# A hybrid decoder layer on one core: the first modulation sums on VectorE, gate rows from transposed tiles, sigmoid through tanh, and a new order of instructions

## The chip, the cores and the metric

The kernel runs on one core of one Trainium2 chip. The metric is the device time of one execution in microseconds (us); lower is better. Engines are named as in the profile: PE is TensorE's matrix multiply (PEld its weight load), DVE is VectorE, ACT is ScalarE, POOL is GpSimd, SP the engine that issues the loads.

## The reference, cut to what matters

One decoder layer in float32, with 512 tokens of width 1024 and one conditioning vector c of width 1024:

```python
mod = silu(c) @ ada_w + ada_b                      # 6 x 1024
sh1, sc1, g1, sh2, sc2, g2 = split(mod, 6)
h = rms_norm(x, pre_norm_mix) * (1 + sc1) + sh1
y = hybrid_mixer(h, ...)                           # input projection, RG-LRU group, sparse attention group, output projection
x = x + (1 + g1) * rms_norm(y, post_norm_mix)
h = rms_norm(x, pre_norm_mlp) * (1 + sc2) + sh2
x = x + (1 + g2) * rms_norm(relu(h @ w_ff1) ** 2 @ w_ff2, post_norm_mlp)
# inside the RG-LRU group, elementwise per channel and token, xc = causal conv of a projection of h:
r, i = sigmoid(xc @ wa + ba), sigmoid(xc @ wx + bx)      # block-diagonal weights
log_a = -8 * r * softplus(-lam)
u = sqrt(-expm1(2 * log_a)) * (i * xc)                   # then the scan h_t = exp(log_a) * h_(t-1) + u_t
```

## The kernel before, in words

Nearly all products are float32 through fp32r: each operand is split into a high and a low part (`hi`, `lo`), and three products replace one (`mm3`). VectorE, ScalarE and POOL make these parts, so they are busy throughout.

**Opening** (`first_wave`, `norm_x`, `ada_load`, `ada_sums`). Four loads bring x, 128 tokens each. ScalarE sums the squares, POOL makes the root, and x is scaled in pieces. `sil`, the silu of c, is broadcast to all partitions by eight small plain fp32 products with `ident` and two copies; the result is `silb`. Sixteen loads bring the tiles of `ada_w` for shift and scale, two per block of 128 channels. For block j `ada_sums` makes a shift and a scale column (`sa`): for j = 0 (`PE_SUMS = 1`) by 16 one-column products on TensorE, for the others by `tensor_tensor_reduce` on VectorE, multiplying the transposed tile by `silb` and summing along the row. Then four transposes, the modulated tile on ScalarE (`hh`, and once more `hf`), the low part `hl` on VectorE, and 18 products of 512 columns into six banks. So the first wave is eight blocks, each with two sums on VectorE. `WARM` plain products on x stand in TensorE's queue before it.

**Middle.** Projections for the RG-LRU and the queries, the compressed keys, and attention run interleaved. `gates` makes r and i (sigmoid on ScalarE out of PSUM); `vector_work` runs the convolution, the decay (tanh, exponential, square root), the scan, the gelu and the group's norm. `ada_row` makes the row (1 + g) * gain for the residual: per half of 512 columns `ada_sum` accumulates eight row tiles, each scaled by a column of `sil`, into `accT` on VectorE; POOL adds the bias on one partition; a product with `ones` sums over the partitions; VectorE multiplies by the gain. It runs for g1 beside the attention and for g2 (stream `G2`) beside the first MLP product.

**End.** `turn_h` and `up_first`, the up projection (`up`, partly by a Strassen scheme), the down projection (`down_all`) with the last residual.

**What sets the order.** Every operation is recorded as a node in the order in which the generator functions make it, then `flush` issues all of them in the order of `PLAN`, a string with one position per node. Each engine works through its own queue in that order. Where an operation may run on several engines, the letter of `PLACE` says which (a ScalarE, d VectorE, p POOL). `TABLES` (line 54) lists which activation tables hold a function: tanh in those of exp, sigmoid and gelu, sigmoid only in its own. In the profile most operations have a helper's line: L334 products, L337 transposes, L344 activations, L376 VectorE and POOL operations, L418 loads.

Of the kernel before, what the change touches and what calls it, by code (L numbers as in the profile page):

```python
# [14 lines left out]
P = 128  # L15
S = 512
# [21 lines left out]
WARM = 16  # L38
# [7 lines left out]
OPENING = "0123AAwAAwAA"  # L46

PE_SUMS = 1
# [27 lines left out]
    '-4-;-=-@-C+?+@,>,L,8,<,:,j-E-F-I+B+C+d+v+r+~+e+l,}-*---K-9-]-^-g-5-J-L-N-P-Q-V-X-Y-f-j-~.0.4.;.@.h-6'
    '-:->-R-W-a-A-T-}..-Z-[-_-c-e-n-q-r-t.b/</W,H,J,X,],O,U-v-x-|+{,#,&,a.$.(.*.-./.6.^.l/y.?.A.E.F.P.Q.Z'
    '.v/&04/b0*01-`.#.,.1.3.8.H.~//-p-y.&.5.M.U.9.:.V.j,e,f-M-h-O-m,;,K-G-b-s-w/+-z.)-{.+.>.W.e.k.m.o.{/:'
    '/c/p-d-i-u.%.2.B-l-o.7.R.i.q.r.s/)/8.t.x.y/5/?/F.<.=.J.g._.u.D.G.L.n.}/./U/Z/6/2/1/>/A/B/J/K/D/H/Y/_'
    '/N/`/f/h.|/(/,/I/4/C.d.f.p.z/k/n0-0S0U/O/P/^/e/m0:/l/o/r/t0D0N/=/@/Q/]/L/T/%/0/S/g/q/{0?0(0//}0@0>/~'  # L80
    '0H0f0g0a0c0m0s0h0p0r0t/a/w0#0+0u0w191L1Y0`0d0n0o0v1+0y0z0~1$1.1F0)020A0G11121=1?101416171_1x1@1T1^1g'
    '1P1R1r1|0=0B1w2V2W2X2Y2]2j3;3>0T0Z0X0^0]0b0I1(0i0x080<0R0M1*1#0j.I.K.N1>1A1H1O.S.T.Y1W1:1f1a.[.`.a1n'
# [1801 lines left out]
```

## Time and profile before

| | |
|---|---|
| time, median of 3 runs (lowest to highest) | 611.64 us (611.56 to 612.51) |
| the profiled execution's own time | 612.0 us |
| its span, first to last instruction | 610.2 us |
| busy: PE, DVE, ACT, POOL | 96%, 92%, 66%, 27% of the span |
| HBM traffic | 86.36 MB read, 2.10 MB written |
| mean granted clock of TensorE | 0.995 |

The span is what the profile's views cover; about 1.8 us of the execution's time lie around it. A busy share is an average over stages with different limits, and the busy time of products is modelled, so idle time of PE is read by stretches. The granted clock is a share of full speed.

### The profile page before, as it was taken

The page shows a single profiled execution, that of the slowest core. Times are in us where ns is not written, and L with a number is a line of the kernel's source. Part 1 is how long each engine was busy: PE and PEld are TensorE (multiplying, and loading weights), DVE is VectorE, ACT ScalarE, POOL GpSimd, SP SyncE. Part 2 cuts the span into 40 slices and gives each one's busy share as a digit, 9 for nine tenths or more (in the row PEclk, how much of TensorE's full clock was granted, in tenths as well). Part 3 has the DMA queues.
Part 4 walks back from the last instruction along what each step waited for, and adds up shares of the span by engine and source line. Part 5 has one row for each costly group of instructions (what it writes and reads, how often), then busy time and mean ns, then how long its engine had stood idle before and what let it go on. Part 6 is the DMA issues. An engine that isn't in the chain of part 4 may idle for free.

```text
span 610.2 us, 10061 instructions
## 1 busy us (share of the span) xinstructions
PE 588.3 (96%) x3500; PEld 511.5 (84%) x3500; DVE 560.2 (92%) x1160; ACT 405.7 (66%) x827; POOL 163.3 (27%) x183
## 2 busy tenths in 40 slices
PE   6999999999989999999999999999989999999994
PEld 6788988977768889879999999998868887888883
DVE  6998989998999899888999998999899999999877
ACT  6646327799999999896757656554476666665322
POOL 5002011246523648530031314133100000221142
PEclk9999999999999999999999999999999999999998
DMA  8994896130155121022253242425324434533303
GB/s 350 386 410 171 329 375 244 70 140 2 69 173 207 35 71 35 0 70 70 104 190 114 95 142 102 154 73 207 120 86 130 148 123 155 171 126 122 133 2 136
DMA packets 26986, 89.10 MB, mean 146 GB/s; under 512 B 2996, under 2 KB 3508, under 8 KB 26936
## 3 DMA queue, kind: packets, MB, share of 16 engines
q1 hardware_dynamic: 26792, 88.40, 41.0%
q8 instruction: 27, 0.44, 0.3%
q14 instruction: 23, 0.19, 0.1%
q10 hardware_dynamic: 144, 0.07, 0.0%
HBM read 86.36 MB, written 2.10 MB: 145 GB/s over the span
## 4 chain that ended last, share of the span: by engine, by line
PE 79%; DVE 12%; ACT 6%; issue 1%; DMA 1%; POOL 0%; POOLq 0%; DVEq 0%; ACTq 0%
PE f L334 25%; PE s L334 19%; PE pv L334 18%; PE tp L334 14%; PE tp L337 4%; DVE r L376 2%; DVE p L376 2%; DVE fT L376 1%; ACT r L344 1%; ACT p L344 1%; DVE lo_C L376 1%; ACT L344 1%; DVE fl L376 1%; ACT junk L344 1%; ACT h L344 1%
## 5 line engine op out<-in xcount | busy, mean ns | idle before, releaser
L344 ACT ACTIVATE p<-p,mx 128x32 f32<-128x32 f32 (+4 forms) x96 | 45.2, 474 | 5.9 <-DVE mx L376 5.7
L334 PE MATMUL f<-hi_o,h 128*128 128x512 f32 x128 | 46.5, 413 | 0.4 <-ACT r L344 0.4
L344 ACT ACTIVATE hi_B<-raw_A 128x512 fp32r<-128x512 f32 x33 | 20.7, 629 | 30.7 <-DVE raw_A L376 22.3
L334 PE MATMUL pv<-pt,V 128*128 128x256 f32 x160 | 37.2, 303 | 2.0 <-DVE pt L376 2.0
L337 PE MATMUL tp<-ident,p 128*128 128x128 f32 x192 | 37.7, 273 | 0.0
L376 DVE TENSOR_TENSOR pt<-tp,pt 128x512 fp32r<-128x512 f32 (+1 forms) x56 | 33.8, 609 | 3.5 <-ACT pt L344 3.0
L334 PE MATMUL s<-K,Q 128*128 128x288 f32 (+4 forms) x128 | 34.8, 335 | 1.4 <-DVE mx L376 1.3
L344 ACT ACTIVATE fT<-fT 128x512 f32<-128x512 f32 x51 | 31.0, 624 | 4.8 <-DVE fT L376 4.1
L376 POOL TENSOR_SCALAR p<-p,den 128x32 f32<-128x32 f32 (+4 forms) x36 | 30.4, 855 | 12.0 <-DVE den L376 7.4
L334 PEld LDWEIGHTS pv<-pt,V 128*128 128x128 f32 x160 | 26.6, 189 | 6.1 <-DVE pt L376 2.8
L344 ACT ACTIVATE hi_D<-raw_d 128x1024 fp32r<-128x1024 f32 x14 | 14.8, 1060 | 22.0 <-DVE raw_d L376 11.4
L376 DVE CUSTOM_DVE_ANT_0 p<-p,silb 128x1024 f32<-128x1024 f32 x23 | 28.6, 1261 | 0.0
L344 ACT ACTIVATE junk<-r 128x1024 bf16<-128x1024 f32 (+2 forms) x21 | 17.9, 851 | 16.1 <-DVE r L376 16.0
L337 PEld LDWEIGHTS tp<-ident,p 128*128 128x128 f32 x192 | 24.6, 140 | 4.0 <-issue 1.0
L334 PEld LDWEIGHTS f<-hi_o,h 128*128 128x128 f32 x128 | 22.9, 188 | 4.2 <-ACT r L344 0.7
L334 PEld LDWEIGHTS s<-K,Q 128*128 128x128 f32 x128 | 22.1, 189 | 4.9 <-DVE mx L376 2.2
L344 ACT ACTIVATE pt<-tp 128x512 fp32r<-128x512 f32 (+1 forms) x44 | 23.2, 533 | 3.6 <-PE tp L337 2.4
L334 PE MATMUL f<-lo_o,h 128*128 128x512 f32 x64 | 25.1, 407 | 0.0
L376 POOL TENSOR_TENSOR fl<-fT,fh 128x512 fp32r<-128x512 f32 x2 | 4.1, 2064 | 78.0 <-ACT fh L344 70.6
L344 ACT ACTIVATE hi_e<-raw_e 128x1024 fp32r<-128x1024 f32 x14 | 14.8, 1058 | 15.0 <-PE s L334 6.6
L334 PE MATMUL f<-third,hi_B 128*128 128x256 f32 x96 | 23.4, 284 | 0.0
L334 PE MATMUL tp<-r,hi_B 128*128 128x256 f32 x96 | 22.9, 284 | 0.1
(422 smaller groups left out, 2318.1 us busy)
## 6 DMA issues: line engine op xcount, KB each, us to landing
p<-in_ada_a SPq DMA_DIRECT2D x16, 512.0 KB, 7.1
ar<-in_ada_r SPq DMA_DIRECT2D x16, 512.0 KB, 3.6
p<-in_ada_t SPq DMA_DIRECT2D x16, 512.0 KB, 5.8
raw_d<-in_wd SPq DMA_DIRECT2D x14, 512.0 KB, 3.1
raw_e<-in_wd SPq DMA_DIRECT2D x14, 512.0 KB, 3.3
raw_A<-in_wf SPq DMA_DIRECT2D x12, 512.0 KB, 4.0
raw_B<-in_wf SPq DMA_DIRECT2D x12, 512.0 KB, 3.3
r<-in_x SPq DMA_DIRECT2D x8, 512.0 KB, 6.9
```

The costliest lines, as they stand in the source:

```text
L334: lambda: self.nc.tensor.matmul(out, lhs, rhs, start=start, stop=stop))
L337: self.issue("pe", 0.109, [out], [src], lambda: self.nc.tensor.transpose(out, src, ident))
L344: return "act", cost, lambda: self.nc.scalar.activation(out, src, func, scale=scale, bias=bias, **kw), func
L376: return eng, cost, lambda: fn(out, *args, **kw), None
```

## The change

- `PE_SUMS` goes from 1 to 0: block 0 of the first wave gets its sums by `tensor_tensor_reduce` on VectorE, like blocks 1 to 7. `WARM` goes from 16 to 10.
- `ada_row` uses transposed tiles too: eight tiles of 128 output columns by 1024 inputs, each one `tensor_tensor_reduce` with `silb`, with bias plus 1 (`ab1`) as start value, into a column of `col`; then four products with `ident` per half broadcast the columns into a row in PSUM, and VectorE multiplies by the gain. `accT`, the bias loads and POOL's adds go. `silb` is therefore needed to the end, and two tiles t2 of the down projection, which were its halves, become tiles of their own.
- r and i: sigmoid(z) = (1 + tanh(z / 2)) / 2. ScalarE makes tanh with scale 0.5 and half the bias (`hb`); the 1 + goes into a `scalar_tensor_tensor` on VectorE for i (four, before four multiplies placed on POOL or VectorE) and into bias columns of the decay's tanh and exponential; the halves go into the constants of `sp4` and the scale of the square root.
- `PLAN` and `PLACE` are new throughout.

```diff
-WARM = 16
+WARM = 10
-OPENING = "0123AAwAAwAA"
-PE_SUMS = 1
+OPENING = "AA0123wAAwAA"
+PE_SUMS = 0
...
-    accT = raws.tile([P, 512], F32, name="accT")
+    t2 = [raws.tile([P, 512], F32, name="t2_0")]
-    t2 = [silb[:, half(0)], silb[:, half(1)]]
...
     def gates():
+        hb = const.tile([P, 8], F32, name="hb")
+        dve("tensor_scalar", hb, col2[:, V_BA:V_BX + 4], 0.5, None, op0=ALU.mult)
...
-                act(dst[:, c4, :512], ps, AF.Sigmoid, bias=col2[:, vb + c4:vb + c4 + 1])
+                act(dst[:, c4, :512], ps, AF.Tanh, scale=0.5, bias=hb[:, vb - V_BA + c4:vb - V_BA + c4 + 1])
...
-    def ada_row(part, dst, gain, brow):
+    def ada_row(part, dst, gain):
         for n in range(2):
             load(dst[n], bass.AP(tensor=gain.tensor, offset=gain.offset + 512 * n, ap=[[0, P], [1, 512]]))
+        col = const.tile([P, 8], F32, name=f"row{part}")
         for n in range(2):
-            acc = yield from ada_sum(part, n)
-            load(brow[0:1, :512], inp["ada_b"][0:1, part * D + n * 512:part * D + n * 512 + 512])
-            yield lambda: clk.ready(acc, brow[0:1, :512])
-            pool("tensor_add", acc[0:1, :], acc[0:1, :], brow[0:1, :512])
-            yield lambda: max(clk.ready(acc), bank_free("tp"))
+            for j in range(4 * n, 4 * n + 4):
+                raw = ar_tile()
+                load(raw, inp["ada_r"][8 * (part == 5) + j])
+                yield lambda: clk.ready(raw)
+                dve("tensor_tensor_reduce", raw, raw, silb, 1.0, ab1[:, 8 * part + j:8 * part + j + 1], ALU.mult, ALU.add,
+                    col[:, j:j + 1])
+            yield lambda: max(clk.ready(col), bank_free("tp"))
             ps = bank("tp")
-            mm(ps, ones, acc, True, True)
-            dve("scalar_tensor_tensor", dst[n], ps, 1.0, dst[n], op0=ALU.add, op1=ALU.mult)
+            for j in range(4):
+                mm(ps[:, tok(j)], col[:, 4 * n + j:4 * n + j + 1].to_broadcast([P, P]), ident, True, True)
+            dve("tensor_mul", dst[n], ps, dst[n])
...
-        dve("tensor_scalar", sp4[:, 0, :], res, 4.0, None, op0=ALU.mult)
-        dve("tensor_scalar", sp4[:, 1, :], res, -8.0, None, op0=ALU.mult)
+        dve("tensor_scalar", sp4[:, 0, :], res, 2.0, None, op0=ALU.mult)
+        dve("tensor_scalar", sp4[:, 1, :], res, -4.0, None, op0=ALU.mult)
...
-            either("tensor_mul", it[:, ct, :512], it[:, ct, :512], xc[:, ct, :512], usual="p")
+            dve("scalar_tensor_tensor", it[:, ct, :512], it[:, ct, :512], 1.0, xc[:, ct, :512], op0=ALU.add, op1=ALU.mult)
...
-            act(tt[:, ct, :512], rt[:, ct, :512], AF.Tanh, scale=sp4[:, 0, ct:ct + 1])
+            act(tt[:, ct, :512], rt[:, ct, :512], AF.Tanh, scale=sp4[:, 0, ct:ct + 1], bias=sp4[:, 0, ct:ct + 1])
...
-            act(rt[:, ct, :512], rt[:, ct, :512], AF.Exp, scale=sp4[:, 1, ct:ct + 1])
+            act(rt[:, ct, :512], rt[:, ct, :512], AF.Exp, scale=sp4[:, 1, ct:ct + 1], bias=sp4[:, 1, ct:ct + 1])
...
-            act(tt[:, ct, :512], tt[:, ct, :512], AF.Sqrt)
+            act(tt[:, ct, :512], tt[:, ct, :512], AF.Sqrt, scale=0.25)
...
-    b5row = clk.lone(fp, [P, 512], F32, name="b5row")
+    t2.append(clk.lone(fp, [P, 512], F32, name="t2_1"))
```

**The opening by the two `PLAN` strings**, as each engine's queue has it (the positions, sorted; the nodes of the opening counted through the code; A0 and A1 are the two `ada_w` tiles of block 0, w0 its projection weights, sq the squares):

```
loads  before: x0 x1 A0 x2 A1 x3 w0 w1 A2 A3 A5 A4 w3 w2 ...
       after:  x0 x1 x2 x3 A1 A0 w0 A3 A2 w1 A5 A4 w2 w3 ...
DVE    before: ctab ident tab, sil (3 operations), ctab2 ... tab2 ... sa0 (2), lo_a0, sum 1.0, hl0, sum 1.1, sa1 ...
       after:  ctab ident tab tab2 ctab2, sil (3, softplus operations between), ... copy of silb, sum 0.1, sum 0.0,
               sa0, scale of x0, lo_a0, sum 1.1, hl0, sa1, sum 1.0, lo_a1, sum 2.1 ...
PE     before: 3 warm, silb and warm mixed, 16 one-column products with warm and transposes between, 4 warm, block 0 ...
       after:  silb (8), 3 warm, transpose, 5 warm, transpose, 2 warm, 2 transposes of block 0, 4 of block 1, block 0 ...
ACT    after:  sil, sq0, softplus exp, sq1, scale, sq2, sq3, scale, copy of silb, 4 scales, hi_a0, hh0 (2), hf0 ...
```

**`PLACE`, letters counted** (a / d / p, before to after), for the streams that change most: opening norm XN 7/5/0 to 9/1/2; weight splits WS 159/269/30 to 166/261/31; after the wave AW 5/6/5 to 6/3/7; scores AS 40/27/45 to 44/30/38; RG-LRU VW 0/10/9 to 0/6/9 (the four multiplies i * xc no longer have a choice; before three of them stood on POOL and one on VectorE; of the four multiplies by the gelu, POOL has three for one, and of the four scalings four for three); TH 15/31/2 to 14/28/6; UP 67/25/8 to 64/27/9; DN 68/104/13 to 69/106/10.

## Rows read from the trace of the kernel before

**Rows 1.** The page: its first line with the span, and its first part (busy time, share of the span and instructions of each engine).

```profile
span 610.2 us, 10061 instructions
...
PE 588.3 (96%) x3500; PEld 511.5 (84%) x3500; DVE 560.2 (92%) x1160; ACT 405.7 (66%) x827; POOL 163.3 (27%) x183
```

**Rows 2.** Busy time by stage. Each line: start and end of the stretch, its length, busy time of each engine (PE, PEld, DVE, ACT, POOL) with its instructions in brackets, then the granted clock of TensorE (1.00 is the whole), the mean busy share of the DMA engines and GB/s.

```profile
20.00:30.00 10.00, 9.80 (x48) 7.71 (x47) 9.93 (x20) 6.48 (x9) 0.00 (x0) 1.00 1.02 407
30.00:40.00 10.00, 10.00 (x49) 8.04 (x48) 9.97 (x18) 3.79 (x6) 0.00 (x0) 1.00 1.03 415
...
125.00:150.00 25.00, 24.93 (x117) 17.60 (x116) 21.91 (x61) 24.46 (x49) 10.98 (x12) 1.00 0.17 64
150.00:175.00 25.00, 22.32 (x114) 17.76 (x113) 24.55 (x59) 23.17 (x54) 10.78 (x10) 1.00 0.40 132
175.00:200.00 25.00, 24.11 (x130) 19.38 (x129) 23.16 (x68) 24.07 (x67) 8.84 (x10) 1.00 0.40 143
...
400.00:450.00 50.00, 48.90 (x283) 42.26 (x282) 47.03 (x83) 27.09 (x49) 10.74 (x9) 1.00 0.38 132
```

**Rows 3.** Instructions in order of time, 4.7 to 22.1 us, all engines: start, length, engine, line, operation, out<-in, shape and count, and in brackets the idle time before with what ended it. A plain fp32 product shows as two records.

```profile
4.68 1.62 PE L334 MATMUL s<-r,ident 128*128 128x128 f32 x6 [4.68 <-DMA r<-in_x]
...
6.08 0.17 DVE L376 TENSOR_TENSOR sil<-sil,vecs 128x8 f32<-128x8 f32 x1
...
6.31 2.93 PE L334 MATMUL tp<-ident,sil 128*128 128x128 f32 x12
...
9.03 1.41 PE L334 MATMUL s<-r,ident 128*128 128x128 f32 x6
...
12.12 0.68 DVE L376 TENSOR_TENSOR tab<-tab,p 128x512 f32<-128x512 f32 x1
...
13.18 1.62 PE L334 MATMUL tp<-sil,p 128*128 128x1 f32 x14
...
15.87 0.21 DVE L376 SCALAR_TENSOR_TENSOR sa<-tp,ab,vecs 128x1 f32<-128x1 f32 x1
...
15.98 1.06 PE L334 MATMUL s<-r,ident 128*128 128x128 f32 x8
...
16.06 0.95 DVE L376 TENSOR_TENSOR lo_a<-raw_a,hi_a 128x768 fp32r<-128x768 f32 x1
16.18 1.02 ACT L344 ACTIVATE h<-tp,sa 128x256 fp32r<-128x256 f32 x2
...
17.25 0.50 PE L334 MATMUL f<-h,hi_a 128*128 128x512 f32 x1 [0.22 <-ACT h L344]
...
18.40 0.69 DVE L376 TENSOR_TENSOR h<-pt,h 128x512 fp32r<-128x512 f32 x1
...
20.40 1.22 DVE L376 CUSTOM_DVE_ANT_0 p<-p,silb 128x1024 f32<-128x1024 f32 x1
20.58 0.78 ACT L344 ACTIVATE pt<-tp,sa 128x512 f32<-128x512 f32 x1 [2.31 <-DVE sa L376]
...
22.07 0.50 PE L334 MATMUL s<-h,hi_a 128*128 128x512 f32 x1 [0.20 <-ACT h L344]
```

**Rows 4.** Queues of the opening. The last line of the view of the tiles r in the first 20 us (for the four loads of x: least, median and most time from issue to landing), and one stretch, columns as in rows 2.

```profile
DMA to landing us min/median/max: 4.6/6.1/7.6
...
8.00:10.00 2.00, 2.00 (x11) 2.00 (x11) 0.40 (x3) 1.15 (x3) 0.42 (x3) 1.00 1.03 424
```

**Rows 5.** ScalarE alone in order of time, 128 to 145 us, columns as in rows 3.

```profile
128.41 1.28 ACT L344 ACT_TABLE_LOAD   x1
129.71 0.69 ACT L344 ACTIVATE r<-s,vecs 128x512 f32<-128x512 f32 x1
...
140.02 0.69 ACT L344 ACTIVATE r<-s,vecs 128x512 f32<-128x512 f32 x1 [0.17 <-PE s L334]
140.73 1.28 ACT L344 ACT_TABLE_LOAD   x1
142.02 1.95 ACT L344 ACTIVATE r<-r,sp 128x512 f32<-128x512 f32 x3
...
144.36 0.60 ACT L344 ACTIVATE p<-p,mx 128x384 f32<-128x384 f32 x1
```

**Rows 6.** The chain that ended last, 140 to 178 us: start, length, what (of its pieces, three).

```profile
160.89 1.39 ACT p L344 x8
...
164.73 3.24 DVE r L376
...
177.92 0.46 PE s L334
```

**Rows 7.** VectorE's and POOL's groups by shape: line, engine, operation, out<-in, shapes, count, then busy us, mean ns of one, and idle before.

```profile
L376 DVE CUSTOM_DVE_ANT_0 p<-p,silb 128x1024 f32<-128x1024 f32 x23 | 28.6, 1261 | 0.0
...
L376 DVE SCALAR_TENSOR_TENSOR accT<-ar,sil,accT 128x512 f32<-128x512 f32 x28 | 21.4, 765 | 0.2
...
L376 DVE SCALAR_TENSOR_TENSOR r<-r,r 128x512 f32<-128x512 f32 x4 | 2.5, 679 | 0.0
...
L376 DVE TENSOR_SCALAR accT<-ar,sil 128x512 f32<-128x512 f32 x4 | 1.9, 482 | 0.1
...
L376 POOL TENSOR_TENSOR r<-r,r 128x512 f32<-128x512 f32 x4 | 5.4, 1368 | 6.8 <-DVE r L376 6.8
```

**Rows 8.** POOL alone in order of time, one row at 164 us, columns as in rows 3.

```profile
164.48 2.40 POOL L376 TENSOR_TENSOR lo_o<-raw_o,hi_o 128x1024 fp32r<-128x1024 f32 x1
```

More of the change, by code (lines that the diff above doesn't have):

```diff
@@ new lines @@
+    '###(#*#7#&#:#c#2#;#>#B#I#Q#U#X#`#s#D#H#L#b#l#.#-#$#%#)#,#/#4#0#@#n#e#g#i#o#w#z#{#~$$$&$)#5#8#<#G$/$='
+    '#?#F#K#t#R#j#N#[#^#u$#$B#Z#m#p#|#x%$$(#y$.$?$+#v$%$,$-$0$4$7$D#q#}$*$1$;$E$N$@$8$C$:$G$P$F$>$U$<$K$T'
+    '$`$L$W$M$J$9$I$S$V$2$3$5$6$R$X$g$H$Q$i$q$Z$h$a$f$]$r$_$y$t$m$k$w$o$~%2${$p$l$[$d$v$e$A$O$^$c$u$z%-$b'
+    '$s%@%*%&%,%4%#%.%+%)%0%7%%%/%E%B%6%?%A%5%1$|%8%:%C$j$x$}%;%>%D%P$n%(%H%K%V%O%G%I%R%M%[%S%d%e%U%l%c%_'
+    '%h%g%^%9%F%T%L%Q%3%<%=%Y%]%b%i%J%X&V%o%j%w&#%q%y%p%s%}&*%r%|&7%t&.&+%x&6%n%`%m%N%Z%a%k%v%z&%%f&-&Y&9'
@@ L185 @@
          'FA': 'ppppppppppdp',
-         'RS': 'ppappaddaddd',
-         'TH': 'aadpdddddaddaaddaaddddpdaaddaadddaddaddaddaddddd',
+         'RS': 'ppppdaddaddd',
+         'TH': 'aadddapdaaddddddadppddppaaddaadddaddaddaddadddpd',
          'UF': 'adad',
-         'UP': 'adadaaddaadpaaaaappaaaaaddaaaaaddaaaaaddaaaaaddaaaaaddaaaaaddaaaaadpaaaadppdaaaaddaaaaappdaaaadd'
+         'UP': 'adadaadpaaddddaaappaaaaaddaaaaadpadaaaddaaaaadpadaaaddaaaaaddadaaaddaaaaapdaaaaappaaaaapdadaaadd'
           'aaaa',
-         'G2': 'dd',
@@ L595, in block_kernel @@
     const = ctx.enter_context(tc.tile_pool(name="const", bufs=1))
-    const.tile([P, 88], F32, name="fill")
+    const.tile([P, 64], F32, name="fill")
     wts = ctx.enter_context(tc.tile_pool(name="wts", bufs=1))
@@ L1148, in gain_split @@
         either("scalar_tensor_tensor", lo, src, gcol, hi.bitcast(F32), op0=ALU.mult, op1=ALU.subtract)
-    def ada_sum(part, n):
-        tiles = []
-        def fetch(k):
-            raw = ar_tile()
-            clk.hold(raw)
-            raw = raw.rearrange("p (k c) -> p k c", k=2)
-            load(raw, inp["ada_r"][8 * (part == 5) + 4 * n + k].rearrange("p (k c) -> p k c", k=2))
-            tiles.append(raw)
-        fetch(0)
-        acc = accT
-        for k in range(KD):
-            if k % 2 == 0 and k // 2 + 1 < KD // 2 and part == 2:
-                fetch(k // 2 + 1)
-            if k % 2 == 0 and k and part == 5:
-                fetch(k // 2)
-            raw = tiles[k // 2][:, k % 2, :]
-            yield lambda: clk.ready(raw)
-            if k == 0:
-                either("tensor_scalar", acc, raw, sil[:, 0:1], None, op0=ALU.mult)
-            else:
-                either("scalar_tensor_tensor", acc, raw, sil[:, k:k + 1], acc, op0=ALU.mult, op1=ALU.add)
-            if k % 2:
-                clk.release(raw)
-        return acc
@@ L1206, in ada_cols @@
         yield after("yp")
-        yield from ada_row(2, late["g1"], inp["post_norm_mix"], h_tile(F32))
+        yield from ada_row(2, late["g1"], inp["post_norm_mix"])
         events.add("g1")
@@ L1850, in lay @@
         "ada_t": np.stack([ada[:, c0:c0 + P].T for c0 in range(3 * D, 5 * D, P)]),
-        "ada_r": np.stack([rows(ada[k:k + 256, c0:c0 + 512]) for part in (2, 5) for c0 in (part * D, part * D + 512)
-                           for k in range(0, D, 256)]),
-        "ada_b": v["ada_b"],
+        "ada_r": np.stack([ada[:, c0:c0 + P].T for part in (2, 5) for c0 in range(part * D, part * D + D, P)]),
         "wcol": np.stack([rows(w) for w in wcol]),
```

243 lines of the change are left out of this document (118 added, 125 removed).

## Prediction, made before the change was run

> **What bounds the kernel now.** I read the page first, then the busy time by stage, then the chain that ended last, and last the order of time where that chain leaves TensorE. The page says TensorE is busy for 588.3 of 610.2 us [rows 1]. So no change off TensorE shortens the kernel except where TensorE stands. What counts is its idle time, and there are two places that this change touches.
>
> The first is the opening. The first product of the input projection starts at 17.25 and the projection's second block at 22.07; between the two TensorE has one block's work and little else [rows 3]. The reader should see who holds the second block: ScalarE idles 2.31 us before 20.58 for the modulation sums (sa) of VectorE, which began them only behind the first block's work. From there VectorE is as full as TensorE, 9.93 and 9.97 of 10 us [rows 2].
>
> The second is 140 to 178 us. The chain there does not run through TensorE: ScalarE holds it to 162 and VectorE until TensorE takes over at 177.92 [rows 6]. TensorE idles 0.07, 2.68 and 0.89 us in the stretches 125:150, 150:175, 175:200, while ScalarE is busy for 24.46, 23.17 and 24.07 of 25 [rows 2]. ScalarE loads the sigmoid's table at 128.41 and the exponential's at 140.73, and no exponential of the scores runs before 144.36 [rows 5].
>
> **The opening, worked out.** The change drops the 32 records of one column on TensorE (1.62 us for 14, so 3.7 us) and six warm-up products. They stood before 17.25, partly in idle time, so they are no term themselves. Two multiply-and-sums of 1.22 us join VectorE [rows 3]. I follow the new order listed with the change.
>
> - sil. Two table operations of 0.68 and about 0.28 us and the small operations of the softplus now stand before it, and one of those waits for an exponential that ScalarE issues behind its first square. Before it was ready at 6.25 (6.08 and 0.17) [rows 3]; I put it at 7.1, an estimate.
> - The broadcast of silb: 16 records. Twelve took 2.93 us, so 16 take 3.9 and end at 11.0. The copy out of PSUM, priced by 18.40 (0.69), ends at 11.7 [rows 3].
> - Are the weights there? The last x load was the sixth in the queue. At 424 GB/s from about 2.5 us on [rows 4], six loads of 512 KB take 7.4 us; with 0.9 us for the slower start the sixth is in by 10.8, and no x load took over 7.6 us from its issue. The two ada loads of block 0 now stand fifth and sixth, so 10.8 holds for them as well. That leaves 0.9 us.
> - Two sums and the small operation (2 x 1.22 + 0.21) end at 14.35. The halves of the modulated tile need the four transposes too, and these stand behind 20 warm-up records. Such records came every 0.27 us at 4.68 and every 0.13 at 15.98; the six right behind silb, at 9.03, took 1.41 [rows 3]. In the same place of the new order the warm-ups take 1.41 and 14 x 0.13, the transposes about 0.5: from 11.0 to 14.7, or to 14.1 if none is slow and 15.5 if half of them are. ScalarE's two halves (1.02) end at 15.7 (15.4 to 16.5) and the first product starts at 15.8.
> - Block 1 on VectorE: a scaling of about 0.35, the low half of the weights 0.87 (0.95, next start 0.87 later), sum 1.22, low half of h 0.6, 0.2, sum 1.22: 4.5 us, to 18.9. ScalarE's 0.7 us brings 19.6. TensorE's 18 products follow each other at 0.229 (estimate: 17.25 to 22.07 less the waits and transposes); with 0.3 for transposes they end 4.4 later, at 20.2. So block 1 starts at about 20.2 for 22.07, and from there on TensorE sets the pace, with VectorE at 4.3 us per block against TensorE's 4.6.
>
> Gain 1.9 us. Bounds: nothing, if anything of this is late by as much, and 3.0 if silb is not late at all.
>
> **Sigmoid through tanh.** The kernel's own table list puts tanh beside the exponential, so both loads go: 2 x 1.28 = 2.56 us less on ScalarE. Of the activations that change, eight (tanh and exponential of the decay) gain a second column operand. 0.78 against 0.69 [rows 3, 5] prices that at 0.09, 0.7 us in all. Net 1.9 us less on ScalarE while it holds the chain. On VectorE four multiplies become scalar_tensor_tensor of 0.68 [rows 7], of which one ran there and three on POOL before: +2.0 us. In turn two gated multiplies go to POOL and one scaling does too: -1.8 us by the same 0.68 and about 0.4. Even. TensorE can win at most its idle time there, 3.6 us, and at least nothing. I take 1.9, since the chain passes from ScalarE to VectorE without slack and VectorE's load stays.
>
> A rule and a row. The load at 140.73 starts 0.02 us after the activation before it ended and the next starts 0.01 after it: a switch costs 1.28 here [rows 5]. The Trainium skill, ScalarE: Activation LUTs, section "What ACT_TABLE_LOAD costs", gives 1283 ns and about 1380 ns of drain, 2.66 us per switch. By it the net would be 4.6 us, above TensorE's 3.6 us of idle time, which caps it: 606.1. The trace shows no drain, so the row decides.
>
> **Residual-gate rows.** Before, per part: 14 accumulating operations of 0.765, two scalings of 0.482, so 11.7 us of VectorE, and two bias adds on POOL. After: eight sums of 1.26 and their 0.08 reads, 10.7 us. The final multiply stays one per half. VectorE saves 1.0 us per part, 2 us in all [rows 7]. TensorE exchanges eight records of 512 columns for 32 of 128: the same columns. The bytes loaded are the same (16 x 512 KB); four tiny loads go. All of it lies beside TensorE's work, so I count it at nothing. The ends: in 400:450 VectorE is busy for 47.03 of 50 [rows 2], and each of 8 sums holds its queue 0.46 us longer than one old operation, so +3.7 if each made TensorE wait; -2.0 if all that is saved were on the path. Nothing is nearest, since TensorE idles 1.1 us there and the total falls.
>
> **Places.** By the letters of the new table, VectorE's choices go down by 8 among the weight splits, 4 in the opening norm, 3 each in two others and up by 1 to 3 in five; POOL falls by 7 in the scores and rises by up to 4 elsewhere. By mean costs VectorE comes out a few us lighter of 560.2 [rows 1]. The order of all instructions is new too. I count zero, with 1.8 us to either side (half of TensorE's idle time in the three stretches from 125 to 200).
>
> A row and a rule that speak against it: the scan at 164.73 took 3.24 us on the chain [rows 6] while POOL ran a 2.40 us subtraction from 164.48 to 166.88 [rows 8]. It was held about 2 us. The Trainium skill, SBUF — State Buffer, in "Reading the diagram", says that a VectorE operation with two SBUF inputs and a POOL operation exclude each other for a whole instruction. The trace agrees. Two more multiplies of 1.37 us on POOL [rows 7] could hold scans for 2.7 us more; three fewer multiplies and no bias adds there take away as much. I leave it at nothing.
>
> **Sum.** The profiled execution took 612.0 us, 1.8 around its span; the median of the runs is 0.4 less. 612.0 - 1.9 - 1.9 = 608.2, on the median 607.8.
>
> **Rivals.**
> 1. Only one gain stays: ScalarE's freed time is refilled, or the opening's lead meets VectorE later. For it: both engines above 90% around [rows 2]. Against it: TensorE, at full work, keeps a lead that it has. About 609.7.
> 2. Both fall away, because TensorE's work is unchanged and the new order waits elsewhere: 611.3.
> 3. More than forecast: without the two tables, scores are free to run from 128 to 144 and the whole idle time of 3.6 us goes, with 1 us from a lighter VectorE, 2.7 beyond the sum: 605.1. The page's 2.66 us per switch would put ScalarE's relief, 4.6 us, on this rival's side; the rows, with no gap around the loads, speak against it.
> 4. Slower: TensorE has worked less when the warm-ups come (from 7.1 on instead of 4.68, with six fewer of them) and keeps its slow pace. The granted clock reads 1.00, the 2.4 GHz level [rows 4], in a stretch whose records still come every 0.24 us, and the pace rises only after work without a pause from 4.68 on [rows 3]. Twenty records at 0.27 then end at 16.4, the transposes at about 18, and the first product comes at 19.2, 2 us late. If one whole block (4.1 us of products) also ran at half pace, 4 more follow. It decides where the first product comes after about 19.2, since from there the 1.9 us of the tables don't pay for it. Some 613.7. Against it: behind silb, in the same place, all but six records came at 0.13.
>
> The change not doing what it says (tanh getting a table of its own) falls under 1: ScalarE would show the ten loads it has.
>
> **Numbers.** Forecast 0.45, rival 1 0.17, rival 2 0.13, rival 3 0.10, rival 4 0.15. A measurement of this kernel tells about 0.2% (1.2 us) from no change. Forecast, 1 and 3 are faster, 0.72; 2 is the same, 0.13; 4 is slower, 0.15. The forecast's own range is 605.8 to 609.8. For 8 in 10 the range leaves out most of rival 4 and the far end of 3: 604.0 to 611.6.
>
> **What would show it.** Right: first product of the projection at 15.4 to 16.6 and second block near 20.2; eight table loads, none between 128 and 140; POOL without accT. Wrong: a first product after 17, TensorE idle above 3 us in 125:200, or VectorE waits of TensorE in 400:450 that were not there.

## The result

The kernel after takes 608.87 us (median of 6 runs, 608.66 to 609.26) against 611.99 for the kernel before beside it (6 runs, 611.56 to 612.51): ratio 0.995, interval 0.9938 to 0.9963. Faster, as forecast: 3.1 us against the 3.8 put, 1.1 above the forecast of 607.8 and inside its range. The profiled execution took 608.91, its span is 606.8. (Lines of code are 3 lower than before: L331 products, L334 transposes, L341 ScalarE, L373 VectorE and POOL; in the kernels of the experiments they are a few lines off either.)

The page of after, as [rows 1]:

```profile
span 606.8 us, 10017 instructions
...
PE 581.1 (96%) x3480; PEld 507.0 (84%) x3480; DVE 553.1 (91%) x1154; ACT 413.6 (68%) x838; POOL 158.6 (26%) x179
```

Busy time by stage of after, columns as in [rows 2]:

```profile
125.00:150.00 25.00, 24.29 (x116) 17.51 (x115) 21.91 (x63) 24.39 (x46) 10.28 (x10) 1.00 0.07 26
150.00:175.00 25.00, 21.20 (x109) 16.73 (x107) 24.27 (x56) 23.54 (x57) 7.83 (x5) 1.00 0.22 76
175.00:200.00 25.00, 23.97 (x143) 20.79 (x144) 23.77 (x75) 24.39 (x67) 9.88 (x13) 1.00 0.64 241
400.00:450.00 50.00, 49.90 (x290) 43.60 (x288) 47.01 (x84) 30.09 (x52) 9.40 (x9) 1.00 0.50 169
```

The opening of after in order of time, columns as in [rows 3]:

```profile
6.44 0.17 DVE L373 TENSOR_TENSOR sil<-sil,vecs 128x8 f32<-128x8 f32 x1
...
6.66 3.56 PE L331 MATMUL tp<-ident,sil 128*128 128x128 f32 x16 [6.66 <-DVE sil L373]
10.05 0.83 PE L331 MATMUL s<-r,ident 128*128 128x128 f32 x6
...
13.56 0.21 DVE L373 SCALAR_TENSOR_TENSOR sa<-sa,ab,vecs 128x1 f32<-128x1 f32 x1
...
13.87 1.02 ACT L341 ACTIVATE h<-tp,sa 128x256 fp32r<-128x256 f32 x2 [0.85 <-DVE sa L373]
...
14.94 0.50 PE L331 MATMUL s<-h,hi_a 128*128 128x512 f32 x1 [0.19 <-ACT h L341]
...
19.20 0.39 PE L331 MATMUL f<-h,hi_a 128*128 128x512 f32 x1
19.43 0.39 PE L331 MATMUL pv<-h,hi_a 128*128 128x512 f32 x1
```

The first product starts at 14.94 for 17.25; 19.20 is the eighteenth, the last of block 0, and the nineteenth follows 0.23 later without a wait, where before the second block began at 22.07 after a wait of only 0.20 [rows 3]. So block 1 starts 2.6 us earlier: 2.3 of them lie ahead of the first product and 0.3 within block 0. The lead of after over before, by the last record of the same products in both traces: 2.9 us at the end of the first wave (55.01 to 52.15), 1.9 at the gates (139.99 to 138.05), 1.7 at the output projection (267.47 to 265.73), 4.3 at the last product (602.08 to 597.77), 3.4 of span. So the opening gave more than put; 125 to 200, where I expected the second gain, gave back over 1 us (TensorE idles 5.5 us there for 3.6); and something I had counted at nothing came behind it. From the first product to the last TensorE stands 8.8 us in both kernels: what it loses at 125 to 200 it wins back later, 1.7 of it at 440 to 460. Of the 4.3 us, 2.3 are the earlier first product; the other 2.0 are busy time, which is modelled, and their cause stays open.

The waits of TensorE in before, 125 to 200 us: who waited for what, us in total, times, longest.

```profile
PE pv L334 <- DVE pt L376: 2.0, 2, 1.7
PE s L334 <- DVE mx L376: 0.9, 1, 0.9
PE f L334 <- ACT r L344: 0.6, 2, 0.4
```

The same of after:

```profile
PE pv L331 <- DVE pt L373: 3.1, 3, 1.4
PE s L331 <- DVE mx L373: 1.1, 1, 1.1
PE f L331 <- ACT r L341: 0.6, 1, 0.6
```

In both it is VectorE that TensorE waits for, but for 0.6 us. The waits of TensorE in before, 425 to 465 us:

```profile
PE tp L334 <- DVE g2row L376: 1.0, 1, 1.0
PE pv L334 <- ACT hi_D L344: 1.0, 1, 1.0
```

In after one is left there:

```profile
PE tp L331 <- DVE g2row L373: 0.4, 1, 0.4
```

Here some 1.7 us are won (TensorE is busy for 19.64 of 20 us in 440:460, before 17.98).

### The profile page after: what moved, and what is told of

It reads as the page before. It is cut to its first block, busy times and chain, and to the rows that moved or that the text cites. A ratio compares the mean times of both kernels' runs of the same rounds, so it can differ in the third digit from the quotient of the medians.

```text
span 606.8 us, 10017 instructions
## 1 busy us (share of the span) xinstructions
PE 581.1 (96%) x3480; PEld 507.0 (84%) x3480; DVE 553.1 (91%) x1154; ACT 413.6 (68%) x838; POOL 158.6 (26%) x179
## 4 chain that ended last, share of the span: by engine, by line
PE 77%; DVE 12%; ACT 4%; issue 3%; DMA 2%; POOLq 0%; POOL 0%; DVEq 0%; ACTq 0%
PE f L331 25%; PE s L331 18%; PE pv L331 18%; PE tp L331 13%; PE tp L334 4%; DVE lo_D L373 3%; DVE fl L373 2%; DVE raw_D L373 1%; DMA raw_D<-in_wd 1%; ACT r L341 1%; ACT p L341 1%; DVE r L373 1%; DVE fS L373 1%; DVE ar L373 1%; DVE raw_d L373 1%
## 5 line engine op out<-in xcount | busy, mean ns | idle before, releaser
L341 ACT ACTIVATE p<-p,mx 128x32 f32<-128x32 f32 (+4 forms) x96 | 45.2, 473 | 3.2 <-DVE mx L373 2.9
L331 PE MATMUL f<-hi_o,h 128*128 128x512 f32 x128 | 46.0, 405 | 0.0
L331 PE MATMUL pv<-pt,V 128*128 128x256 f32 x160 | 37.3, 309 | 2.3 <-DVE pt L373 2.3
L341 ACT ACTIVATE hi_B<-raw_A 128x512 fp32r<-128x512 f32 x36 | 22.7, 630 | 23.1 <-DVE raw_A L373 13.2
L334 PE MATMUL tp<-ident,p 128*128 128x128 f32 x192 | 36.7, 273 | 0.7 <-DVE pt L373 0.5
L373 DVE TENSOR_TENSOR pt<-tp,pt 128x512 fp32r<-128x512 f32 (+1 forms) x56 | 33.8, 609 | 2.7 <-ACT pt L341 2.1
L331 PE MATMUL s<-K,Q 128*128 128x288 f32 (+4 forms) x128 | 34.8, 332 | 1.2 <-DVE mx L373 1.1
L373 POOL TENSOR_SCALAR p<-p,den 128x32 f32<-128x32 f32 (+4 forms) x30 | 26.0, 877 | 26.4 <-DVE den L373 25.0
L331 PEld LDWEIGHTS pv<-pt,V 128*128 128x128 f32 x160 | 27.0, 189 | 7.0 <-DVE pt L373 2.9
L341 ACT ACTIVATE fT<-fT 128x512 f32<-128x512 f32 x47 | 28.7, 625 | 5.3 <-DVE fT L373 4.8
L373 POOL TENSOR_TENSOR fl<-fS,fh 128x256 fp32r<-128x256 f32 x4 | 3.2, 794 | 104.2 <-DVE fl L373 68.4
L373 DVE CUSTOM_DVE_ANT_0 p<-p,silb 128x1024 f32<-128x1024 f32 x24 | 29.7, 1244 | 0.1
L334 PEld LDWEIGHTS tp<-ident,p 128*128 128x128 f32 x192 | 24.4, 141 | 5.7 <-DVE pt L373 1.5
L341 ACT ACTIVATE pt<-tp 128x512 fp32r<-128x512 f32 (+1 forms) x45 | 24.1, 538 | 5.4 <-PE tp L334 3.2
L341 ACT ACTIVATE junk<-r 128x1024 bf16<-128x1024 f32 (+2 forms) x21 | 17.9, 851 | 13.9 <-DVE r L373 13.4
L341 ACT ACTIVATE hi_D<-raw_d 128x1024 fp32r<-128x1024 f32 x14 | 14.8, 1060 | 17.7 <-DVE raw_d L373 10.8
L331 PEld LDWEIGHTS f<-hi_o,h 128*128 128x128 f32 x128 | 23.4, 188 | 2.8
L331 PEld LDWEIGHTS s<-K,Q 128*128 128x128 f32 x128 | 22.0, 189 | 4.5 <-DVE mx L373 1.5
L331 PE MATMUL f<-lo_o,h 128*128 128x512 f32 x64 | 25.5, 403 | 0.0
L331 PE MATMUL pv<-r,hi_B 128*128 128x256 f32 x96 | 23.4, 286 | 0.1
L331 PE MATMUL f<-h,hi_g 128*128 128x512 f32 x64 | 22.6, 406 | 0.6 <-ACT r L341 0.6
L331 PE MATMUL f<-third,hi_B 128*128 128x256 f32 x96 | 23.0, 283 | 0.0
```

The source lines that it names most:

```text
L331: lambda: self.nc.tensor.matmul(out, lhs, rhs, start=start, stop=stop))
L334: self.issue("pe", 0.109, [out], [src], lambda: self.nc.tensor.transpose(out, src, ident))
L341: return "act", cost, lambda: self.nc.scalar.activation(out, src, func, scale=scale, bias=bias, **kw), func
L373: return eng, cost, lambda: fn(out, *args, **kw), None
```

## The experiments

Theory: the opening sets the gain; from 140 to 200 VectorE's queue is the bound, so ScalarE's relief is worth little and what VectorE carries there decides. Rivals: ScalarE is the bound there; the parts are worth their price in any order; the new order does it alone. First each part alone in before's order, then parts undone or moved in after.

**Tanh alone, in the order of before.** The change's lines for r, i and the decay, with before's nodes and order; the three products that stood on POOL run on VectorE.

```diff
-act(dst, ps, AF.Sigmoid, bias=col2)
+act(dst, ps, AF.Tanh, scale=0.5, bias=hb)
-tensor_mul(it, it, xc)                      # three on POOL
+nc.vector.scalar_tensor_tensor(it, it, 1.0, xc, op0=ALU.add, op1=ALU.mult)
```

> The kernel before with only the sigmoid taken through tanh: same order, same places, except that the four products of the input gate (three of them on GpSimd before) are scalar_tensor_tensor on VectorE. Theory A (the term of the forecast: ScalarE holds the chain from 140 to 178 us, so two table loads less, net 1.9 us, arrive at the end): the loads at 128.4 and 140.7 are gone, TensorE's idle time in 125:200 falls from 3.6 to about 1.7 us, ratio near 0.997. Rival B (VectorE is as full as ScalarE there and sets the pace, so ScalarE's relief changes nothing): idle time in 125:200 stays at 3 to 4 us, ratio 0.999 to 1.001, with both loads gone all the same.

613.49 (613.24 to 614.99) against 611.88: ratio 1.0032 (1.0019 to 1.0044). VectorE of this kernel in order of time:

```profile
141.01 0.69 DVE L1265 SCALAR_TENSOR_TENSOR r<-r,r 128x512 f32<-128x512 f32 x1
...
144.69 0.69 DVE L1265 SCALAR_TENSOR_TENSOR r<-r,r 128x512 f32<-128x512 f32 x1
...
145.89 0.55 DVE L376 CUSTOM_DVE_ANT_1 p<-s,tab 128x384 f32<-128x384 f32 x1
```

Its stretch 140:145, columns as in [rows 2]:

```profile
140.00:145.00 5.00, 4.10 (x26) 3.21 (x25) 4.91 (x14) 3.71 (x7) 0.31 (x1) 1.00 0.00 0
```

The same stretch of before:

```profile
140.00:145.00 5.00, 4.94 (x33) 3.81 (x31) 4.93 (x18) 4.95 (x8) 3.98 (x4) 1.00 0.00 0
```

Both loads are gone, and ScalarE stands for 1.3 of 5 us instead of working. VectorE is full in both; its three new operations (two of them shown) push the row maxima (the last row of the first fence, at 143.86 in before) 2.0 us back. Here VectorE's queue set the time, and not ScalarE's. Both theories had these operations at nothing, so the run doesn't show what the relief of ScalarE is worth by itself.

**The same with those products on POOL**, as an add and a multiply.

```diff
-nc.vector.scalar_tensor_tensor(it, it, 1.0, xc, op0=ALU.add, op1=ALU.mult)
+nc.gpsimd.tensor_scalar(it, it, 1.0, None, op0=ALU.add)
+nc.gpsimd.tensor_mul(it, it, xc)            # three of four
```

> As the run with the sigmoid alone taken through tanh, but the three products of the input gate that GpSimd had stay there, each as an addition of one (about 0.6 us) and a product (1.4 us); VectorE has no more work than before. It asks what two table loads less on ScalarE are worth by themselves. Theory A (VectorE is the bound of that stretch, ScalarE's relief is worth nothing; the 2 us lost in the other run were the three operations of 0.69 us on VectorE): same as before within 0.7 us, ratio 0.999 to 1.001. Rival B (the forecast's term: 1.9 us): ratio near 0.997. Rival C (GpSimd's longer operations hold VectorE): slower, ratio 1.001 or more.

615.35 (615.0 to 615.72), ratio 1.0056 (1.0044 to 1.0069). A wait of ScalarE in 140:152:

```profile
ACT r L344 <- POOL r L1268: 3.7, 1, 3.7
```

VectorE and POOL of this kernel in order of time:

```profile
145.27 2.36 DVE L376 SCALAR_TENSOR_TENSOR p<-r,r 128x512 f32<-128x512 f32 x2
...
146.03 1.93 POOL L1267 TENSOR_SCALAR r<-r 128x512 f32<-128x512 f32 x1
```

POOL's chain is late and ScalarE waits 3.7 us for it; and two VectorE operations that took 1.29 in before take 2.36 beside POOL. TensorE in turn waits 1.9 us for ScalarE's r, for 0.6 in before. So the price only went from VectorE to POOL, and the relief by itself is not shown here either. (The opening has the low clock of the next run; behind it the same product comes 0.2 us later than in before, so it is little of the loss.)

**The rows alone, in the order of before.**

```diff
-either("scalar_tensor_tensor", acc, raw, sil[:, k:k + 1], acc, op0=ALU.mult, op1=ALU.add)   # 8 per half
+nc.vector.tensor_tensor_reduce(w, w, silb, 1.0, ab1, ALU.mult, ALU.add, row[:, j:j + 1])    # 4 per half
```

> The kernel before with only the residual-gate rows by multiply-and-sum of transposed tiles: same order; each sum stands in the place of the second of the two accumulating operations that it replaces, the bias adds on GpSimd and their four small loads are gone. Theory A (the forecast: all of it is hidden): ratio 0.999 to 1.001. Theory B (from the two traces: before, TensorE waits 1.0 us for VectorE's product with the gate row and 1.0 us for ScalarE's split of a weight behind it, between 440 and 460 us; after, 0.4 us in all): the waits there fall by 1 to 2 us, ratio 0.997 to 0.998. Rival C (a sum of 1.27 us holds VectorE's queue longer than one old operation): new waits of TensorE in 150:200 or 400:460, ratio above 1.001.

617.26 (616.0 to 617.67), ratio 1.0085 (1.0071 to 1.0099). Two places. First the opening, which this edit does not touch: a stretch, columns as in [rows 2].

```profile
16.00:18.00 2.00, 2.00 (x8) 1.66 (x8) 2.00 (x5) 1.78 (x4) 0.00 (x0) 0.51 1.01 382
```

Two of its products in order of time:

```profile
17.79 0.63 PE L334 MATMUL pv<-h,hi_a 128*128 128x512 f32 x1
18.21 0.63 PE L334 MATMUL f<-h,lo_a 128*128 128x512 f32 x1
```

The clock falls to its lower level (1.2 GHz) though TensorE has not stood still, and products come every 0.43 us for 0.23. It costs little: the first product came 0.5 us earlier here, part of the rest goes into a wait that before has there, and behind the stretch the same product comes 0.3 us later than in before. Second, VectorE and POOL of this kernel in order of time:

```profile
119.13 2.59 POOL L376 TENSOR_TENSOR lo_g<-raw_g,hi_g 128x1024 fp32r<-128x1024 f32 x1 [5.29 <-ACT hi_g L344]
119.42 2.33 DVE L376 TENSOR_SCALAR eg<-eg 128x24 f32<-128x24 f32 x1
```

The same two operations in before:

```profile
118.50 0.17 DVE L376 TENSOR_SCALAR eg<-eg 128x24 f32<-128x24 f32 x1
...
118.74 2.40 POOL L376 TENSOR_TENSOR lo_g<-raw_g,hi_g 128x1024 fp32r<-128x1024 f32 x1 [5.30 <-ACT hi_g L344]
```

An operation of 24 columns, 0.17 us, came 0.24 us ahead of POOL's subtraction in before; here it comes 0.29 behind and is held for all of it, and TensorE then waits 2.1 us for a transposed copy. Of the 3.3 us that this execution ends later, the opening makes 0.3 and this hold 2.3; the rest, and the 1.3 us by which the median lies above this execution, the trace does not explain. The waits at 440 to 460 stay as in before (1.0 and 0.9), so what after wins there is not the rows' alone.

**A later opening.** Four products of 0.69 on VectorE ahead of block 0's sums in after.

```diff
+for _ in range(2): nc.vector.tensor_mul(t2[0], w[:, half(0)], silb[:, half(0)])   # ahead of each sum
```

> The changed kernel with four products of 128x512 (about 0.69 us each, 2.7 us, result unused) on VectorE ahead of the two sums of block 0, so that the first product of the projection comes at about 17.6 instead of 14.9. Theory A (the lead of the opening is carried to the end one to one, since TensorE sets the pace from block 1 on): 2.3 to 2.8 us slower than the changed kernel, about 611.4, ratio to before 0.999. Rival B (the lead is lost again where TensorE waits for VectorE and ScalarE, between 140 and 180 us, so it is worth little at the end): under 1.2 us slower than the changed kernel, about 609.5, ratio 0.996 to 0.997.

613.28 (612.75 to 614.25), ratio 1.0023 (1.0013 to 1.0034). The last transposes and the first product of this kernel in order of time:

```profile
17.09 0.66 PE L339 MATMUL tp<-ident,r 128*128 128x128 f32 x4 [3.24 <-DVE r L378]
17.94 0.50 PE L336 MATMUL s<-h,hi_a 128*128 128x512 f32 x1 [0.19 <-ACT h L346]
```

A later stretch:

```profile
20.00:22.00 2.00, 2.00 (x6) 1.52 (x5) 2.00 (x5) 1.64 (x3) 0.00 (x0) 0.50 1.02 416
```

The first product comes 3.0 us later, and since the clock is at its lower level until about 22, after TensorE has stood 3.24 us, block 0 loses 1.6 more. Of these 4.6 us, 4.4 are there at the end: the delay goes through one to one. The opening's lead is real time. (The new opening alone, in before's order, was not run.)

**After without its ten warm-up products.**

```diff
-mm(wave[3][:, 0:P], ident, xt[0][:, P:2 * P], True, True)
```

> The changed kernel without its ten warm-up products (20 records; TensorE then has nothing between the broadcast of silb, to 10.2, and the transposes). It tells what the warm-ups are worth, and so what the slower rival of the forecast was about. Theory A (without them TensorE's clock is at the lower level when the projection begins): products of block 0 every 0.43 us for some us, granted clock near 0.5 there, 2 to 4 us slower than the changed kernel, ratio to before 0.998 to 1.002. Rival B (the level depends on the broadcast alone, or rises at once): transposes earlier, first product at 14.9 as before since the sums hold it, no difference.

610.79 (610.0 to 612.41), ratio 0.9986 (0.9978 to 0.9994). A stretch of this kernel:

```profile
16.00:18.00 2.00, 2.00 (x7) 1.52 (x6) 2.00 (x5) 2.00 (x3) 0.00 (x0) 1.00 1.02 413
```

Two products of the same stretch:

```profile
16.27 0.63 PE L331 MATMUL pv<-h,lo_a 128*128 128x512 f32 x1
16.70 0.63 PE L331 MATMUL s<-h,lo_a 128*128 128x512 f32 x1
```

The first product comes 0.3 late, but block 0 goes at 0.43 a product until 19.48. The warm-ups are worth 1.9 us. The clock's row reads 1.00 throughout, so the pace is the better witness.

**Gelus in one group.** After spreads four gelus in three groups between exponentials, so it loads tables 11 times, before 10. Two gelus moved to the third: 9 loads. (In each pair the first node goes behind the second, or ahead of it where that is negative.)

```diff
+MOVES = ((1370, -1371), (1372, -1371), (1374, 1370), (1376, 1372), (1297, 1371), (1294, 1297), (1378, 1294))
```

> The changed kernel with the first two of the four gelu operations (and what reads them) moved behind the scores, next to the third: nine table loads instead of eleven, 2.56 us less on ScalarE between 150 and 165 us. Theory A (the split of the gelus into three groups, which the new order brought, eats what the sigmoid's loads gave): TensorE's idle time in 125:200 falls from 5.5 to about 3.5 us, 1.5 to 2 us faster than the changed kernel, ratio to before near 0.992. Rival B (VectorE, busy for 4.5 to 5.0 of every 5 us there, sets the pace): within 0.6 us of the changed kernel, ratio 0.994 to 0.996.

610.23 (609.79 to 611.81), ratio 0.9978 (0.9969 to 0.9987): 1.4 above after. Two stretches of this kernel:

```profile
150.00:160.00 10.00, 10.00 (x53) 8.42 (x52) 9.71 (x23) 6.84 (x26) 0.00 (x0) 1.00 0.06 11
160.00:170.00 10.00, 6.57 (x34) 4.77 (x32) 7.60 (x22) 9.18 (x22) 5.11 (x4) 1.00 0.40 148
```

VectorE's wait in the second:

```profile
DVE h L381 <- ACT h L349: 2.3, 1, 2.3
```

ScalarE has 3 us free and TensorE is full for ten microseconds: until 165 us the same products come 1.4 us earlier than in after. Then the later group holds h, VectorE stands 2.3 us in its busiest stretch with row maxima queued behind, and from 167 on they come 1.1 us later. So ScalarE's relief does reach TensorE, but this order loses more than it wins.

**Four sums of g1 earlier** (from 157 to 176 to 110 to 131):

```diff
+MOVES = ((1427, 825), (1430, 1427), (1425, 947), (1428, 1425), (1469, 1029), (1429, 998))
```

> The changed kernel with the first four of the eight sums of the mixer's residual-gate row (1.27 us each on VectorE, at 157.8, 164.1, 171.7 and 174.1 us) and two of their loads moved to between 110 and 131 us, where VectorE stood idle for some 5 us waiting for TensorE and ScalarE. Nothing else is moved. Theory A (VectorE sets the pace from 145 to 180 us, so 5.1 us less on it there is time won): TensorE's idle time in 150:180, 4.8 us in the changed kernel, falls to 2.5 or less; 2 to 3 us faster than the changed kernel, about 606.5, ratio to before 0.990 to 0.992. Rival B (ScalarE's table loads set it, VectorE only follows): within 0.6 us of the changed kernel, ratio 0.994 to 0.996. Rival C (the sums are in the way in their new place): TensorE waits for VectorE between 110 and 135 us, slower than the changed kernel.

610.29 (609.17 to 611.42), ratio 0.9974 (0.9964 to 0.9983). Two stretches, which in after read 9.42 and 7.71 of TensorE:

```profile
140.00:150.00 10.00, 8.22 (x38) 6.86 (x38) 8.79 (x37) 8.53 (x21) 3.09 (x6) 0.83 0.00 1
...
160.00:170.00 10.00, 9.84 (x50) 8.06 (x49) 9.41 (x26) 9.91 (x27) 3.25 (x3) 1.00 0.52 168
```

Where the sums leave, TensorE wins 2.1 us; where they come, the row maxima come 2.4 us later and more is lost, a clock of 0.83 with it. Most of this delay is one sum. It in order of time, with POOL:

```profile
129.85 2.40 POOL L381 TENSOR_TENSOR lo_g<-raw_g,hi_g 128x1024 fp32r<-128x1024 f32 x1 [2.73 <-PE f L339]
130.16 3.18 DVE L381 CUSTOM_DVE_ANT_0 ar<-ar,silb,ab 128x1024 f32<-128x1024 f32 x1
```

It begins 0.31 us behind POOL's subtraction and takes 3.18 us for its usual 1.28.

**The end.** The statistic and its power earlier: 

```diff
+MOVES = ((5406, -5373), (5422, 5373), (5423, 5422))
```

> The changed kernel with two small operations of the last row's statistics and GpSimd's power moved ahead of a product and a scaling of 512 columns in VectorE's queue. In the changed kernel 5.6 us lie between TensorE's last product and VectorE's last operation, before the change 4.9. Theory A (the new order put the power at 600.4, 1 us behind the square that it needs): VectorE ends about 0.6 us earlier, ratio to before 0.993 to 0.995 against 0.995. Rival B (VectorE's 4.9 us of work behind the last product set the end, whatever their order): no difference over 0.2 us.

609.33 (608.82 to 610.27), ratio 0.996 (0.9949 to 0.9972): nothing. The power comes only 0.2 us earlier (600.21 for 600.41) and the end stays, which fits rival B. Why after's end is 0.9 us longer than before's stays open.

**One sum into a gap.** VectorE waits 1.97 us for transposes behind 128 in after; one sum goes there.

```diff
+MOVES = ((1427, 998), (1430, 1427))
```

> The kernel after with one of the eight sums of g1 moved from 157.8 to the place behind 128.1, where VectorE waits 1.97 us for transposes, and its buffer's next load right behind it. Theory (the sums cost where VectorE is the bound, and cost nothing in a gap): VectorE is 1.3 us lighter at 157 to 176, TensorE waits less there: 0.5 to 1.3 us under the kernel after, 607.6 to 608.4. Rival (any operation put in front of the scores delays them, as with four sums): 0 to 1 us over the kernel after.

608.1 (607.54 to 609.09) against 611.9, ratio 0.9938 (0.9925 to 0.9951). The moved sum in order of time:

```profile
128.97 1.28 DVE L381 CUSTOM_DVE_ANT_0 ar<-ar,silb,ab 128x1024 f32<-128x1024 f32 x1
```

A stretch in which TensorE was busy for 7.71 in after:

```profile
160.00:170.00 10.00, 8.68 (x44) 6.49 (x42) 9.94 (x24) 9.92 (x25) 4.88 (x3) 1.00 0.22 79
```

About 0.8 under after by the medians, the lowest of all here, though the two intervals overlap. The trace puts it where the theory does: the same products come 0.4 us later than in after until 162 and 0.8 earlier from 164 to the end. And this sum begins ahead of POOL's subtraction (129.99), so it is not held, as one of the four sums was.

**That and the gelus in one group**, with VectorE's two operations that waited for h behind the maxima:

```diff
+MOVES = ((1427, 998), (1430, 1427)) + GELUS + ((1379, 1509), (1387, 1454))
```

> The kernel before it (one sum in the gap) and the gelus in one group (9 loads), with the two operations of VectorE that waited for ScalarE's h now behind the row maxima. Theory (two loads less help where VectorE's queue does not wait behind them): 1 to 2.5 us under the kernel after, 606.4 to 607.9. Rival (ScalarE's relief is worth nothing wherever it falls, VectorE is the bound): within 0.6 us of the kernel with the moved sum alone, or slower since the group of gelus makes POOL's products and h later.

610.48 (610.06 to 611.19), ratio 0.9978 (0.997 to 0.9987). VectorE's 2.3 us wait is gone, but the group of gelus is still late for POOL's products, one h is held to 2.20 us (0.74 in after) beside POOL, and TensorE's clock falls, in this stretch:

```profile
170.00:180.00 10.00, 8.70 (x33) 6.70 (x33) 9.25 (x17) 8.17 (x18) 2.48 (x2) 0.66 0.42 145
```

At 167 the same products come 1.8 us earlier than in after, from 183 on 2.5 later. Two loads less did not help in the two orders tried; whether another order would keep what they win is open.

**Rows undone in after.** In the new order each sum becomes two accumulating operations in the same place, and one product with ones; the bias of the two rows is left out.

```diff
-dve("tensor_tensor_reduce", raw, raw, silb, 1.0, ab1[...], ALU.mult, ALU.add, col[:, j:j + 1])
+for k in range(2): nc.vector.scalar_tensor_tensor(acc, raw[:, half(k)], sil[...], acc, op0=ALU.mult, op1=ALU.add)
```

> The kernel after with the residual-gate rows as before in the new order: each sum of 1.27 us becomes two accumulating operations of 512 columns (0.48 to 0.77 each) in the same place of VectorE's queue, and four products per half become one product with ones. The bias of the two rows is left out. Theory (the rows are worth little by themselves, and they cost what VectorE pays where it is the bound, 157 to 196): VectorE pays 0.2 to 0.3 us more per sum, 8 sums between 157 and 190, so about 2 us more there and nothing at g2: 1.0 to 2.5 us over the kernel after, 610 to 611.5. Rival A (the rows are worth nothing either way): within 0.6 us of the kernel after. Rival B (long operations hold the queue, short ones are better): up to 2 us under the kernel after.

612.12 (611.27 to 613.56), ratio 1.0008 (0.9999 to 1.0017): 3.2 above after. (Seven runs lie at 611.3 to 612.2 and five at 613.4 to 613.6; the profile is of the upper kind, and what the lower kind pays is not shown by row.) VectorE of this kernel in order of time:

```profile
175.87 2.56 DVE L1166 SCALAR_TENSOR_TENSOR silb<-ar,sil,silb 128x512 f32<-128x512 f32 x2
178.35 0.55 DVE L375 CUSTOM_DVE_ANT_0 p<-s,tab 128x384 f32<-128x384 f32 x1
```

TensorE's wait for it and two others, 125 to 200:

```profile
PE s L333 <- DVE mx L375: 3.4, 3, 2.6
```

Two operations that took 1.5 us elsewhere take 2.56 beside POOL, the maximum behind them starts at 178.35 (175.34 in after), and TensorE stands 2.6 us. POOL's operation begins at 176.62, between the two. In after, the multiply-and-sum of the same place begins first, and it is POOL that is held (the same operation took 1.10 us at 179.05):

```profile
174.14 1.28 DVE L373 CUSTOM_DVE_ANT_0 ar<-ar,silb,ab 128x1024 f32<-128x1024 f32 x1
174.97 1.59 POOL L373 TENSOR_TENSOR r<-r 128x512 f32<-128x512 f32 x1 [4.23 <-ACT r L341]
```

One long operation let POOL in behind it; two short ones let it in between.

**Sigmoid back in after.**

```diff
-nc.scalar.activation(dst, ps, AF.Tanh, scale=0.5, bias=hb)
+nc.scalar.activation(dst, ps, AF.Sigmoid, bias=col2)
```

> The kernel after with only the sigmoid back in ScalarE's eight operations on r and i, all in the new order (VectorE multiplies in the same places, no bias columns in the decay). The new order runs the decay's exponentials between the gates, so each change of function costs a load: 19 table loads for 11, eight more between 125 and 141. Theory (tanh is worth what it lets the order do: it is the new order's condition, though alone in the old order it lost): 8 x 1.28 = 10.2 us more on ScalarE, less its idle time of about 1 us and 0.7 us for the eight second operands, so the scores come 7 to 9 us later and a part of it is won back before 200: 613 to 618. Rival (VectorE is the bound there, ScalarE's load is hidden): below 611.

619.99 (619.81 to 620.21), ratio 1.0131 (1.0118 to 1.0144): 11.1 above after. 19 loads, eight more than after, 10.2 us of ScalarE. What TensorE waits for, 100 to 200:

```profile
PE s L333 <- ACT r L1067: 6.6, 2, 5.3
```

It stands for the gates. So the new order, which runs the decay between the gates, stands on tanh; alone, in the old order, neither tanh nor the rows pay. What the new order gives without both was not run.

## Why the prediction was right, and where it was wrong

The sum was right to 1.1 us by errors of both signs, and that is luck: 608.87 lies nearer to rival 1 (609.7), and what rival 1 says, that the opening's lead meets VectorE later, is what came at 125 to 200.

- **Opening, put at 1.9: 2.9.** Mechanism right, size low. sil came at 6.61 (put 7.1) and the six records behind it at 0.14 us (put at 1.41 for the six), so the transposes never limited: sums at 13.8, ScalarE's halves at 14.89, first product at 14.94 (put 15.8), second block at 19.4 (20.2). The wait that I read first, ScalarE's 2.31 us for sa, was of little weight: TensorE itself waited 0.20 there. The later opening shows that such time goes through to the end.
- **Tanh, put at 1.9: not a term of its own.** The two loads went, none between 128 and 140. The step that failed is "I take 1.9": I read ScalarE's share and the chain [rows 2, 6] as its bound, where TensorE's waits name VectorE. Relief of ScalarE is not worth nothing (the gelus in one group won 1.4 us), but in none of the orders tried was it kept to the end. And "Even", by letters of the place table, left out where the operations lie: alone, three of them in VectorE's full queue made the kernel 1.6 us slower. "Eight table loads" was wrong too: I counted functions, not the new order's changes between them; after has 11.
- **Rows, put at nothing with -2.0 to +3.7: in the new order worth 3.2 by the medians,** beyond my lower end; in the old one no gain. The failed step is "all of it lies beside TensorE's work": it looked at where the rows stood in before, while after puts eight sums at 157 to 190, where VectorE holds TensorE. One sum less there is worth about 0.8, within the noise of the medians but located by the trace.
- **Places, put at nothing.** The order can't be had without the parts, nor they without it: undone in the new order they cost 3.2 and 11.1, added to the old one they cost 5.4 and 1.6. A sum over parts priced in the old order had no term for that. (Some of the 5.4 is not explained, as said there.)
- **POOL against VectorE, "I leave it at nothing".** This was the wrong place to stop: the hold of about 2 us on [rows 8] falls on or off an operation with a shift of half a microsecond, and it made 2.1 us of the rows' loss and 1.9 us of one moved sum. The Trainium skill, SBUF — State Buffer, in "Reading the diagram", has the rule for a VectorE operation with two SBUF inputs: whichever of the two engines starts first holds the other for the whole instruction. The runs agree (a sum of 3.18 us for 1.28 behind POOL; POOL's 1.59 for 1.10 behind a sum). They also show an operation with one input held (2.33 for 0.17), which the page has only for a mode that no run shows.
- **Signs.** I named TensorE's idle time above 3 us in 125:200 as a sign of a wrong forecast. It came (5.5), and the time was still right, because the opening and 440:460 paid. Rival 4 did not come: its price, by the later opening and the missing warm-ups, would have been 1.9 to 4.4. Why 440:460 got better is shown only in part: with the rows undone the wait for g2row is 1.0 again and the same products behind it come 0.6 us later; for the other 1.1 us no run shows the cause.

## What to carry to other kernels

An engine at 98% busy (ScalarE here) is not yet what holds TensorE: ask whose operation TensorE's waits name, and price an operation by the stretch it moves into, not by its length. Where a hand-made order changes with the operations, test the parts both ways, added to the old order and taken out of the new one. Look for gaps of the full engine and put work there, but see first whether POOL has begun an operation: who began first decided some 2 us here.

## What the runs showed of the hardware

- In these pairs of VectorE and POOL, whichever began first held the other. Behind POOL subtractions that began 0.3 us earlier, a VectorE operation of 24 columns took 2.33 us (0.17 alone) and a multiply-and-sum 3.18 (1.28 alone); beside POOL, pairs of 512-column operations took 2.36 for 1.29. A multiply-and-sum that began 0.83 us ahead of POOL's operation kept its 1.28, and POOL's took 1.59 (1.10 alone); a maximum that reads PSUM, begun at 175.34 beside that same POOL operation, kept its 0.55.
- The granted clock fell to the lower level in the opening of two kernels, whose opening is that of before, without an idle microsecond of TensorE from 14 to 20 (0.51 and 0.50 in 16:18); before shows no such fall. And it read 1.00 where products came every 0.43 us, the pace of the stretches that read 0.50. The Trainium skill, TensorE: Matmul & The Clock Gate, "Seeing it yourself", warns that clock events of a trace have been unreliable; these rows agree.
